# A Huber loss over 512 MB of inputs: eight added loads from GpSimd, and middle tiles computed in two pieces

## The chip, the cores and the metric

The kernel runs on one core of a Trainium2 chip. The metric is the device time of one execution in microseconds, as a median of several runs. TensorE does nothing here. The work is done by the DMA engines, which move data between HBM and the on-chip memory, by VectorE (DVE in the profile) and by ScalarE (ACT). SyncE (SP) issues the transfers; GpSimd (POOL) only sets four constants before the change.

## The reference

```python
def setup_inputs():
    return {"pred": np.random.randn(8192, 8192).astype(np.float32),
            "target": np.random.randn(8192, 8192).astype(np.float32)}

def reference(pred, target):
    delta = 1.0
    diff = pred - target
    abs_diff = np.abs(diff)
    return np.where(abs_diff <= delta, 0.5 * diff**2, delta * (abs_diff - 0.5 * delta))
```

Two inputs of 268 MB are read, one output of the same size is written, and each element needs a handful of operations.

## The kernel before

The arrays are taken as flat lists of 67 million numbers and cut into 40 tiles of 128 partitions. A tile has 13248 columns; the first and the last have 10432. One row of a full tile, 52992 bytes, lies contiguous in HBM. Two slots `a0`, `a1` hold `pred`, two slots `b0`, `b1` hold `target` and later the result; tile i uses slot i modulo 2.

For each piece of columns of a tile, VectorE subtracts (`a = a - b`, line 82) and clips (`b = clip(a, -1, 1)`, line 83), ScalarE then computes `b = Square(b * sqrt(0.5))` (line 86) and `a = |a|` (line 87), and VectorE ends with `b = max(a - 0.5, b)` (line 76). Since max(|d| - 0.5, clip(d)^2 / 2) is the Huber loss with delta 1, `b` then holds the result. The first halves of the pieces run ahead of the last step: `finish(2)` holds back the last step of two pieces. `PARTS` names the number of pieces of tiles 0 (two), 38 (four) and 39 (eight); all others, tiles 1 to 37, fall to the default in `shares(i, PARTS.get(i, 3))`, three pieces of 4416 columns.

All transfers are issued by SP in the order in which the program has them (`manual_schedule`): loads of tile 0, loads of tile 1, and then for each tile i its computation, `store(i)` (line 68) and the loads of tile i + 2 (line 49). A middle tile has one load of `a`, one of `b` and one store, 6624 KB each. Tiles 0 and 1 are loaded in halves of their columns (`HALVES`: a, b, a, b); the last two in smaller pieces. SP waits, in order, for what each transfer needs: the store of tile i for the last step of VectorE, the load of `a` for tile i + 2 until slot `a` is no longer read, the load of `b` for tile i + 2 until the store of tile i has left the slot. So while tile i is computed, the loads of tile i + 1 are under way.

Of the kernel before, what the change touches and what calls it, by code (L numbers as in the profile page):

```python
# [1 line left out]

# [4 lines left out]


@with_exitstack
def kernel(  # L10
    ctx: ExitStack,
    tc: tile.TileContext,
    pred: bass.AP,
    target: bass.AP,
    out: bass.AP,
):
    nc = tc.nc
    P = 128
    fp32 = mybir.dt.float32
    Alu = mybir.AluOpType  # L20
    Act = mybir.ActivationFunctionType
    SQRT_HALF = 0.70710678118654752

    total = pred.shape[0] * pred.shape[1] // P
    W = 13248

    ends = total % W + W
    widths = [ends - ends // 2] + [W] * (total // W - 1) + [ends // 2]
    n = len(widths)
    starts = [sum(widths[:i]) * P for i in range(n)]  # L30

    def block(x, i):
        flat = x.rearrange("r m -> (r m)")
        return flat[starts[i] : starts[i] + P * widths[i]].rearrange("(p m) -> p m", p=P)

    pool = ctx.enter_context(tc.tile_pool(name="slots", bufs=1))
    a_slots = [pool.tile([P, W], fp32, name=f"a{k}") for k in range(2)]
    b_slots = [pool.tile([P, W], fp32, name=f"b{k}") for k in range(2)]

    def shares(i, parts):  # L40
        w = widths[i] // parts
        edges = [k * w for k in range(parts)] + [widths[i]]
        return [slice(edges[k], edges[k + 1]) for k in range(parts)]

    def load(i, which, first, last):
        quarters = shares(i, 4)
        c = slice(quarters[first].start, quarters[last].stop)
        dst, src = (a_slots, pred) if which == "a" else (b_slots, target)
        nc.sync.dma_start(out=dst[i % 2][:, c], in_=block(src, i)[:, c])  # L49

    HALVES = (("a", 0, 1), ("b", 0, 1), ("a", 2, 3), ("b", 2, 3))
    LOADS = {
        0: HALVES,
        1: HALVES,
        n - 2: (("a", 0, 2), ("b", 0, 1), ("a", 3, 3), ("b", 2, 3)),
        n - 1: (("a", 0, 2), ("b", 0, 0), ("b", 1, 1), ("b", 2, 2), ("a", 3, 3), ("b", 3, 3)),
    }
    PARTS = {0: 2, n - 2: 4, n - 1: 8}

    def store(i):  # L60
        if i == n - 1:
            eighths = shares(i, 8)
            pieces = [slice(eighths[k].start, eighths[k + 1].stop) for k in (0, 2, 4)]
            pieces += eighths[6:]
        else:
            pieces = shares(i, 1)
        for c in pieces:
            nc.sync.dma_start(out=block(out, i)[:, c], in_=b_slots[i % 2][:, c])

    def compute(i):  # L70
        todo = []

        def finish(keep):
            while len(todo) > keep:
                a, b = todo.pop(0)
                nc.vector.scalar_tensor_tensor(  # L76
                    out=b, in0=a, scalar=-0.5, in1=b, op0=Alu.add, op1=Alu.max
                )

        for c in shares(i, PARTS.get(i, 3)):  # L80
            a, b = a_slots[i % 2][:, c], b_slots[i % 2][:, c]
            nc.vector.tensor_tensor(out=a, in0=a, in1=b, op=Alu.subtract)  # L82
            nc.vector.tensor_scalar(  # L83
                out=b, in0=a, scalar1=-1.0, scalar2=1.0, op0=Alu.max, op1=Alu.min
            )
            nc.scalar.activation(out=b, in_=b, func=Act.Square, scale=SQRT_HALF)  # L86
            nc.scalar.activation(out=a, in_=a, func=Act.Abs)  # L87
            todo.append((a, b))
            finish(2)
        finish(0)  # L90

    ctx.enter_context(tc.manual_schedule())

    def load_all(i):
        for piece in LOADS.get(i, (("a", 0, 3), ("b", 0, 3))):
            load(i, *piece)

    load_all(0)
    load_all(1)
    for i in range(n):  # L100
        compute(i)
        store(i)
        if i + 2 < n:
            load_all(i + 2)


# [1 line left out]
_INS = ['pred', 'target']  # L108
_OUTS = [((8192, 8192), 'float32')]


# [23 lines left out]
```

## Time and profile before

| | |
|---|---|
| time, median of 3 runs | 1868.83 us (1868.62 to 1869.63) |
| the profiled execution: its time, its span | 1869.48 us, 1867.7 us |
| VectorE busy | 1405.9 us, 75% |
| ScalarE busy | 903.7 us, 48% |
| SP's DMA queue, share of 16 engines' time | 99.8% |
| bytes read and written | 536.87 MB and 268.44 MB, 431 GB/s over the span |
| transfers | 134, all from SP |

In the profile a line is named by its number in the kernel, an engine and the tiles out<-in. `SPq` is SP's queue: a line with it is an issue of a transfer, not the transfer. "b<-in_target_dram" is a load of `target` into slot `b`, "out_dram<-b" a store. In the list of instructions in order of time, the columns are the start, the duration, the engine, the line and the operation, and in brackets the idle time before it and what ended it. In the chain of work that ended last the columns are start, duration and what stood on the chain, and the duration of a transfer runs from its issue to its landing, its time in the queue with it. A transfer is split by rows over the sixteen DMA engines, and each engine adds one to the transfer's semaphore when its share has landed: the trace has 16 such increments for each transfer, and their spread tells how far apart the engines are.

### The profile page before, as it was taken

Reading aid. Unit: us, or ns where it says so; the run is one execution under the profiler, and the core shown is the slowest. Engines: PE = TensorE matmul, PEld = TensorE weight load, DVE = VectorE, ACT = ScalarE, POOL = GpSimd, SP = SyncE. Lnnn points to the kernel's source line nnn. Section 1 sums busy time; section 2 is a strip of 40 time slices with the busy share of each in tenths; the row PEclk is TensorE's granted clock in tenths of the full one; section 3 lists DMA queues with packets and bytes.
Section 4 is the critical chain, followed back from the end, with each engine's and each line's share of the span. In section 5 each row is a group of like instructions: output and inputs, shape, how many; then the busy total and the mean of one; then the engine's idle time right before and its main releaser. Section 6 shows DMA issues by size and latency. Waiting matters only on the chain.

```text
span 1867.7 us, 983 instructions
## 1 busy us (share of the span) xinstructions
DVE 1405.9 (75%) x375; ACT 903.7 (48%) x251; POOL 0.2 (0%) x4
## 2 busy tenths in 40 slices
DVE  4877777777777777777777777777777777777796
ACT  4444444444444444444444444444444444444464
POOL 0000000000000000000000000000000000000000
DMA  9999999999999999999999999999999999999998
GB/s 410 432 429 434 432 436 433 435 433 431 431 436 431 436 434 436 435 431 431 434 434 435 435 435 436 435 429 434 434 431 436 434 435 436 435 429 435 430 428 377
DMA packets 19303, 805.37 MB, mean 431 GB/s; under 512 B 2144, under 2 KB 2144, under 8 KB 2400
## 3 DMA queue, kind: packets, MB, share of 16 engines
q1 hardware_dynamic: 19296, 805.31, 99.8%
q14 instruction: 7, 0.06, 0.0%
HBM read 536.87 MB, written 268.44 MB: 431 GB/s over the span
## 4 chain that ended last, share of the span: by engine, by line
DMA 60%; DVE 38%; issue 1%; ACT 0%; DVEq 0%; another core or an unknown queue 0%; SPq 0%
DMA b<-in_target_dram 32%; DMA out_dram<-b 28%; DVE a L82 15%; DVE b L76 15%; DVE b L83 8%; ACT b L86 0%; ACT a L87 0%; DVEq L130 0%; SPq L49 0%; DVEq L82 0%
## 5 line engine op out<-in xcount | busy, mean ns | idle before, releaser
L86 ACT ACTIVATE b<-b 128x4416 f32<-128x4416 f32 (+3 forms) x125 | 461.0, 3688 | 949.7 <-DVE b L83 949.7
L82 DVE TENSOR_TENSOR a<-a,b 128x4416 f32<-128x4416 f32 (+3 forms) x125 | 565.2, 4522 | 442.1 <-DMA b<-in_target_dram 442.1
L76 DVE SCALAR_TENSOR_TENSOR b<-a,b 128x4416 f32<-128x4416 f32 (+3 forms) x125 | 558.5, 4519 | 3.6 <-ACT a L87 3.6
L87 ACT ACTIVATE a<-a 128x4416 f32<-128x4416 f32 (+3 forms) x125 | 460.3, 3682 | 0.0
L83 DVE TENSOR_SCALAR b<-a 128x4416 f32<-128x4416 f32 (+3 forms) x125 | 293.0, 2344 | 4.3
L86 ACT ACT_TABLE_LOAD x1 | 1.3, 1283 | 0.7 <-PEq L119 0.7
L119 POOL MEMSET const-bfloat16-1.0<- 128x1 bf16 x1 | 0.1, 101 | 0.0
L119 POOL MEMSET const-uint8-127<- 128x1 uint8 x1 | 0.1, 101 | 0.0
L119 POOL MEMSET const-float32-0.0<- 128x1 f32 x1 | 0.1, 98 | 0.2 <-issue 0.2
L119 POOL MEMSET const-float32-1.0<- 128x1 f32 x1 | 0.1, 98 | 0.0
## 6 DMA issues: line engine op xcount, KB each, us to landing
out_dram<-b SPq DMA_DIRECT2D x38, 6624.0 KB, 26.9
a<-in_pred_dram SPq DMA_DIRECT2D x36, 6624.0 KB, 42.1
b<-in_target_dram SPq DMA_DIRECT2D x36, 6624.0 KB, 31.3
b<-in_target_dram SPq DMA_DIRECT2D x4, 3312.0 KB, 35.5
a<-in_pred_dram SPq DMA_DIRECT2D x2, 3312.0 KB, 40.5
a<-in_pred_dram SPq DMA_DIRECT2D x2, 2608.0 KB, 14.5
b<-in_target_dram SPq DMA_DIRECT2D x2, 2608.0 KB, 20.3
out_dram<-b SPq DMA_DIRECT2D x1, 5216.0 KB, 21.3
```

What stands on the lines that cost most here:

```text
L76: nc.vector.scalar_tensor_tensor(out=b, in0=a, scalar=-0.5, in1=b, op0=Alu.add, op1=Alu.max)
L82: nc.vector.tensor_tensor(out=a, in0=a, in1=b, op=Alu.subtract)
L83: nc.vector.tensor_scalar(out=b, in0=a, scalar1=-1.0, scalar2=1.0, op0=Alu.max, op1=Alu.min)
L86: nc.scalar.activation(out=b, in_=b, func=Act.Square, scale=SQRT_HALF)
L87: nc.scalar.activation(out=a, in_=a, func=Act.Abs)
L119: nc = _bacc.Bacc("TRN2", target_bir_lowering=False, num_devices=1)
```

## The change

GpSimd gets eight loads, issued by `ahead()` between the loads of tile 0 and those of tile 1. They come in four pairs. The first of a pair reads `low` rows of 16 columns (64 bytes a row), the second `16 - low` rows of 4096 columns (16384 bytes a row), with `low` 8, 10, 12 and 14. Their rows are four partitions apart, and no two of the eight touch the same bytes. They read `pred` for tile 1 into slot `a1`, the same data to the same place that the ordinary loads of tile 1 bring afterwards. Since those write the same bytes, SP now waits with its first load of `a` for tile 1 until the four loads of 4096 columns have landed, and with the second one for the four of 16 columns. The rest of SP's order is as it was.

Tiles 1 to 37 are computed in two pieces of 6624 columns in place of three of 4416, and `finish(1)` holds back the last step of one piece in place of two; tiles 38 and 39 keep their four and eight pieces, but there too a last step now comes one piece sooner in VectorE's order. Tile 0, with two pieces, keeps its order.

```diff
-        for c in shares(i, PARTS.get(i, 3)):
+        for c in shares(i, PARTS.get(i, 2)):
...
             todo.append((a, b))
-            finish(2)
+            finish(1)
         finish(0)
...
+    EXTRA = 4096
+
+    def ahead():
+        for low in (8, 10, 12, 14):
+            high = 16 - low
+            r = low // 2 - 4
+            for first, k, c in ((0, low, slice(W - 16, W)), (96 - 4 * high, high, slice(0, EXTRA))):
+                rows = slice(first + r, first + r + 4 * (k - 1) + 1, 4)
+                nc.gpsimd.dma_start(out=a_slots[1][rows, c], in_=block(pred, 1)[rows, c])
+
     load_all(0)
+    ahead()
     load_all(1)
```

## The prediction

> **What bounds the kernel now.** I read the page first. About 0.2% of 1868.83 us, 3.7 us, is what a measurement of this kernel can tell from no change.
>
> ```profile
> span 1867.7 us, 983 instructions
> DVE 1405.9 (75%) x375; ACT 903.7 (48%) x251; POOL 0.2 (0%) x4
> q1 hardware_dynamic: 19296, 805.31, 99.8%
> ```
>
> SP's queue fills the sixteen DMA engines for 99.8% of the span; VectorE is busy 75%. So the end is set by bytes and by how evenly the sixteen share them. Second, the chain, around one period of two tiles and around the slow early ones:
>
> ```profile
> 151.82 4.77 DVE a L82
> ...
> 246.99 4.77 DVE a L82
> ...
> 341.37 4.77 DVE a L82
> ...
> 435.52 4.77 DVE a L82
> ...
> 1222.72 26.86 DMA out_dram<-b
> 1249.59 31.27 DMA b<-in_target_dram
> 1280.95 4.77 DVE a L82
> ```
>
> One period is store 26.86, load of b 31.27, compute 35.6 (with issue gaps), together 93.85 us from 529 us on. That VectorE stands in this chain is no bound: a store takes 26.86 us only because its bytes wait behind a load; it is a third of a tile's 46.9 us of traffic, 15.6 us. The marks show something else: the first periods are 95.17, 94.38 and 94.15 us. Against 93.85 the slowest DMA engine loses 1.32 + 0.53 + 0.30 = 2.15 us there, then nothing. Two later stores take 27.66 and 27.67 us (from 846.52 and 1504.26) instead of 26.87: 0.8 us each.
>
> Third, the windows at the very end, busy time of all engines in each stretch (last columns: DMA share, GB/s):
>
> ```profile
> 1859.00:1861.00 2.00, 0.00 (x0) 0.00 (x0) 0.00 (x0) 1.00 0.99 404
> 1861.00:1861.50 0.50, 0.00 (x0) 0.00 (x0) 0.00 (x0) 1.00 0.60 240
> 1862.00:1862.50 0.50, 0.00 (x0) 0.00 (x0) 0.00 (x0) 1.00 0.31 125
> 1863.50:1864.00 0.50, 0.00 (x0) 0.00 (x0) 0.00 (x0) 1.00 0.23 94
> 1864.50:1865.00 0.50, 0.00 (x0) 0.00 (x0) 0.00 (x0) 1.00 0.05 21
> 1866.00:1866.50 0.50, 0.00 (x0) 0.00 (x0) 0.00 (x0) 1.00 0.03 10
> ```
>
> All sixteen work until 1861; from 1864.5 on a share of 0.05 is one engine in sixteen. The trace's semaphore increments, sixteen per transfer, say the same: their spread on the first input's loads is 0.65 us, 1.7 by 182 us, 3.0 by 307, 3.5 by 495, 4.5 after 870, 5.5 after 1495 and 5.5 on the last store. Ten engines end within 0.8 us of each other, six trail by 1.6, 2.9, 3.3, 3.5, 4.0 and 5.5. Following packets engine by engine, the trailers lost 0.1 to 0.7 us each time on the last row of a load of b while others turned to the store, until they stood some 2.8 us or more behind; then they lost almost nothing more. The last one also met three 8 KB instruction fetches (the second queue of the page), 0.7 to 0.8 us each, which explains the two long stores. If the work of 1861 to 1866.5 were levelled, it would end near 1862.3 (the shares sum to 1.3 us). So at most some 4 us can be won by levelling, and little beyond that: a row of 52992 bytes takes 1.956 us in nearly every record.
>
> **The change: GpSimd's loads.** The 44 rows of 64 bytes are nothing beside 52 KB rows: the nearest record, 5216 bytes, takes 0.20 us, so an engine with four of them pays between 0 and 0.8 us; by the order below the last pair of engines has none, so I take zero. The big ones are 8 + 6 + 4 + 2 = 20 rows of 16384 bytes, 0.33 MB. One row costs 16384 / 52992 x 1.956 = 0.61 us of one engine. The two transfers of each pair have 16 rows in all. If each row goes to another engine and the next transfer begins where the last ended, the small one takes engines 0 up to its count and the big one the rest: engines 8 and 9 get one big row, 10 and 11 two, 12 and 13 three, 14 and 15 four. That is a ramp of 0.61, 1.21, 1.82 and 2.42 us over eight engines, laid down before the first transition from load to store. The trace has no transfer on fewer than sixteen engines, so this is the assumption that counts; spread evenly the same bytes are 20 x 0.61 / 16 = 0.76 us on each. The Trainium skill ("DMA: Bandwidth & Descriptors", section "Why a DMA increments its semaphore by 16 and not by 1") says that GpSimd's transfers take a divisor of the row count as the number of engines, consecutive from a cursor that goes round, and knows an exception in which some copies use all sixteen; no transfer here can show which holds.
>
> Price of the ramp: the last pair carries 2.42 us of extra work to the end. What it buys: the slips of the trailing engines came while neighbours stood close, and engines far enough apart lost almost nothing for 1300 us. If the ramp does that from the start, the last engine trails by 2.42 plus what instruction fetches add. These become fewer: VectorE goes from 298 to 226 instructions and ScalarE from 253 to 179, SP stays at 131. I allow 0.4 us for one fetch half hidden (0 if it meets a leading engine, 0.8 if the last). So 5.5 us of trail becomes 2.42 + 0.4 = 2.8, a gain of 2.7. Bounds: at best the pack's own early losses go too (below); at worst the slips go on and the ramp adds to them, +2.4.
>
> Queues: the DMAs stand on GpSimd, which does only four memsets (0.2 us). SP's first load of a for tile 1 now waits for the four big ones, its third for the small ones, and SP is in order, so tile 1's b halves, store 0 and everything later are queued behind. The cover: tile 0's four loads keep the engines busy until about 27.7 us (their last increments), and an issue needs 1.2 us to its first packet (0.73 to 1.9 us at the start), so the wait is free if GpSimd's loads have landed by some 26.4 us; each us beyond costs one. SP's own issues take 0.34 to 0.70 us, eight make 2.8 to 5.6 us; 20 rows beside tile 0's rows add a few us at most. I take zero, with the upper end open until GpSimd's start is seen. By the Trainium skill's fit for GpSimd's transfers (same page, section "Anatomy of one DMA — SWDGE (gpsimd) path": 2.0 us each plus bytes), eight in a row would be an estimated 17 us, inside that cover too.
>
> **Two pieces instead of three.** Each of five groups loses 37 instructions, one for each of 37 tiles. From the rows of 4416 and 5216 columns (subtract 4.753 and 5.592, clip 2.459 and 2.876, Square 3.872 and 4.550, Abs 3.867 and 4.533, last step 4.750 and 5.589) a piece of 6624 costs 7.07, 3.61, 5.74, 5.71 and 7.07 us. One tile: subtract and clip to 10.7, ScalarE's first pair to 22.1, VectorE's second pair done at 21.4 (waits 0.8), last step to 29.2; ScalarE's second pair to 33.6, so VectorE waits 4.4; end at 40.7, against 35.6 now. This 5.1 us is on no path while the DMA queue has work:
>
> ```profile
> 1269.64 0.34 SPq L68 DMA_DIRECT2D out_dram<-b  x1
> 1280.95 4.76 DVE L82 TENSOR_TENSOR a<-a,b 128x4416 f32<-128x4416 f32 x1 [11.34 <-DMA b<-in_target_dram]
> ```
>
> The store is issued 11.3 us before the queue's last load lands; with two pieces 6.2 us, still above the 1.2 us of an issue. Gone, it would cost its lack 37 times; I take zero.
>
> The tail has less cover. There VectorE goes on from tile 37 to 38 without a wait (1786.51), and `finish(1)` adds waits for ScalarE: in tile 38 about 0.4 us at the first last step and 2.3 at the fourth (ScalarE's 5.9 us against one last step of 3.6), in tile 39 some 0.2 and 1.1. From the landing of tile 37's b to the last store's issue it is 104.9 us now (1751.01 to 1855.9), by such steps about 111.3 with the change, and 115.5 to the end of the DMA work (1866.5). So the last store, 0.65 MB, has 4.2 us left, and needs 1.2 us to its first packet and 1.6 for eight rows of 0.2: 1.4 us over. I take zero here too, but each us that I have missed beyond 1.4 is a us of time, up to perhaps 3.
>
> Sum: -5.5 + 2.4 + 0.4 = -2.7 us; I keep 0.2 of it back for the tail: -2.5. The profiled execution took 1869.48 us (span 1867.7, 1.8 around it), 0.65 above the median; there I expect a span near 1865.2. From the median: 1868.83 - 2.5 = 1866.3.
>
> **Rivals.** *The whole pack gains.* The leading engine also lost 0.6 us against its own best rows up to 490 us and 0.7 after. If the ramp removes the early slips for all and the last pair meets no fetch: -5.5 + 2.4 - 0.6 - 0.5 (part of the rest) = -4.2, 1864.6. For it: the losses fall on load-to-store turns that sixteen engines made together. Against: eight engines stay in step.
>
> *Tail bound by VectorE.* If the last issue comes 3 us later than worked out, the end moves by 1.6: 1867.9. The 15.6 us of loads that were still queued when tile 38's store was issued (1823.01) speak against a larger hole.
>
> *Bytes only.* GpSimd's rows spread over all engines, the slips stay: +0.76, 1869.6. By the Trainium skill ("DMA: Bandwidth & Descriptors", "Rules for kernel authors") issuing from another engine brings no bandwidth, and transfers under 64 KB are mostly overhead; the trace agrees that the queue is full, at 431 GB/s, but its last 5.5 us show that fullness is not level.
>
> *Ramp on top of slips.* The engines between 1 and 2.8 us behind were those hit; the ramp puts six there. Then 5.5 + 2.4, up to 1871.2.
>
> *GpSimd lands late.* Its first transfer has a start-up cost that no row shows. At 4.5 us for each of eight, they land at 37 us, 10.6 us past the cover: 1866.3 + 10.6 = 1876.9. It decides for slower from a landing at about 33 us (6.3 beyond cover). Against: 26 us are long beside SP's 0.7 us.
>
> **How the numbers follow.** Forecast 0.36; whole pack 0.32; tail 0.06; bytes only 0.03; ramp on top 0.03; late or another loss above 3.7 us 0.20. Faster by over 0.2% is the whole pack's case, 0.32; within it are forecast, tail, bytes and ramp on top, 0.48; slower 0.20. The range runs from 1863.6 (the pack's case with another us) to 1872.5, past the ramp on top; it leaves out most of the late case. The likeliest case's own range is 1865.1 to 1868.
>
> **What would show it.** Right: increments on tile 0's or 1's loads already 2 to 3 us apart and on the last store under 3.5; periods of 93.85 from the first; DMA share at 1.0 until some 2.5 us before the end; VectorE's wait for b near 6.3 us a tile; SP's first wait over before 26 us. Wrong: a spread at the end of 5 us or more, an idle DMA queue between 1855 and 1863, a gap in the DMA share near 28 us, or a wait for b near zero.

## The result and the profile after

The changed kernel takes 1880.87 us (median of 7 executions, 1870.47 to 1884.21) against 1868.83 us before (7 executions, 1868.26 to 1869.63): ratio 1.0058, 95% interval 1.0044 to 1.0071 (all ratios here come from all executions of a kernel, so they need not be the quotient of the two medians). It is slower, outside the forecast's range. Its executions differ by 14 us where those of before differ by 1.4, and the profiled one was the best of them, 1870.47 us. The same kernel run once more (`after_again` below) gave a profile of 1882.92 us, so both kinds can be read.

The page of the changed kernel, best execution:

```profile
span 1868.7 us, 818 instructions
DVE 1401.9 (75%) x264; ACT 896.9 (48%) x177; POOL 4.4 (0%) x12
q1 hardware_dynamic: 19296, 805.31, 99.8%
q0 software_dynamic: 256, 0.33, 0.1%
```

The queue is as full as before, 0.33 MB have come from GpSimd, and VectorE is no busier. Nothing on the page says what the other executions lose. The start, in order of time (start, duration, engine, line and operation), first VectorE's first line before, then the changed kernel:

```profile
15.86 5.59 DVE L82 TENSOR_TENSOR a<-a,b 128x5216 f32<-128x5216 f32 x1 [15.86 <-DMA b<-in_target_dram]
```

```profile
1.25 4.20 POOL L106 DMA_DIRECT2D a<-in_pred_dram  x8 [0.81 <-PEq L141]
...
19.81 5.59 DVE L82 TENSOR_TENSOR a<-a,b 128x5216 f32<-128x5216 f32 x1 [19.81 <-DMA b<-in_target_dram]
21.26 0.33 SPq L49 DMA_DIRECT2D a<-in_pred_dram  x1
```

GpSimd issues its eight loads in 4.2 us, and SP's wait for them is over at 21.26 us, ahead of the 26.4 us at which the queue would have run dry. But VectorE starts at 19.81 where it started at 15.86 before: the first two loads of tile 0 have landed 4 us later.

Now the place that the prediction had costed at nothing, store against next landing, around 1230 us of the best execution:

```profile
1228.66 0.34 SPq L68 DMA_DIRECT2D out_dram<-b  x1
1235.18 7.06 DVE L82 TENSOR_TENSOR a<-a,b 128x6624 f32<-128x6624 f32 x1 [6.55 <-DMA b<-in_target_dram]
```

The store is issued 6.5 us before the next load of b has landed, where it was 11.3; 6.2 had been worked out. Here it is enough. The chain of the long execution (`after_again`; start, duration, what) shows that it is not enough there:

```profile
289.27 22.05 DMA out_dram<-b
311.33 31.32 DMA b<-in_target_dram
...
950.50 22.20 DMA out_dram<-b
972.72 32.42 DMA b<-in_target_dram
...
1045.65 22.04 DMA out_dram<-b
1067.71 32.56 DMA b<-in_target_dram
...
1614.04 23.07 DMA out_dram<-b
1637.13 31.27 DMA b<-in_target_dram
```

A good period has a store of 22.05 and a load of 31.27 us. From 760 us on each period of two tiles is too long by 0.7 to 1.4 us, in the store or in the load; from 950.50 to 1045.65 it is 95.15 us, not 93.85. In the best execution all periods after 437 us take 93.84 to 94.41. The windows (length, busy time of the three engines, clock, DMA share, GB/s), first of the best execution, then of the long one, say the same:

```profile
673.00:860.00 187.00, 140.77 (x25) 90.25 (x16) 0.00 (x0) 1.00 1.00 434
1048.00:1235.00 187.00, 140.91 (x24) 90.25 (x16) 0.00 (x0) 1.00 1.00 433
1423.00:1611.00 188.00, 141.73 (x25) 90.25 (x16) 0.00 (x0) 1.00 1.00 434
```

```profile
110.00:485.00 375.00, 281.34 (x49) 180.50 (x32) 0.00 (x0) 1.00 1.00 434
673.00:860.00 187.00, 141.17 (x24) 90.25 (x16) 0.00 (x0) 1.00 1.00 430
1048.00:1235.00 187.00, 141.18 (x24) 90.25 (x16) 0.00 (x0) 1.00 1.00 429
1423.00:1611.00 188.00, 139.91 (x25) 90.25 (x16) 0.00 (x0) 1.00 1.00 428
```

The DMA share reads 1.00 in all of them: the engines count as busy, and yet move 1% less. So the share does not show the loss; the records of single rows do. The records carry no engine number: a row belongs to the engine whose row before it ended at that moment. The table has, for some tiles, the shortest time from the issue of a store to its first row on any engine, that is, how much queue the leading engine still had:

```
shortest time from a store's issue to its first row, us (profiled executions)
kernel            tile 10   tile 20   tile 30   tile 34   time of that execution
before              7.06      6.24      6.08      5.27    1869.48
after (best)        2.45      2.33      2.17      2.14    1870.47
after_again         2.39      1.59      0.90      0.93    1882.92
two_only            1.95      1.07      1.59      1.83    1881.71
```

About 0.85 us is the least that occurs in any run: then the engine had nothing left and waited for the store. One such place in the long execution, tile 16, whose store is issued at 808.39:

```profile
808.39 0.34 SPq L68 DMA_DIRECT2D out_dram<-b  x1
808.82 0.38 SPq L49 DMA_DIRECT2D a<-in_pred_dram  x1
815.16 7.06 DVE L82 TENSOR_TENSOR a<-a,b 128x6624 f32<-128x6624 f32 x1 [6.80 <-DMA b<-in_target_dram]
```

```profile
807.00:808.00 1.00, 1.00 (x1) 0.00 (x0) 0.00 (x0) 1.00 1.22 530
808.00:809.00 1.00, 0.36 (x1) 0.00 (x0) 0.00 (x0) 1.00 0.49 212
809.00:810.00 1.00, 0.00 (x0) 0.00 (x0) 0.00 (x0) 1.00 1.50 636
```

(A row counts in the slice in which it is recorded, so a share can pass 1.) By VectorE's line the store came 6.8 us ahead of the load's landing. But a landing is the sixteenth increment, that of the last engine. The leading engines were over 5 us ahead of it. The first of them was done with the load 0.54 us after the store's issue, and the first row of the store came 0.86 us after it; ten engines stood still, for 0.24 us on average. That is still the smaller part of the loss, as will be seen: most of it is in rows that take longer.

### The profile page after: what moved, and what is told of

It reads as the page before. It is cut to its first block, busy times and chain, and to the rows that moved or that the text cites. A ratio compares the mean times of both kernels' runs of the same rounds, so it can differ in the third digit from the quotient of the medians.

```text
span 1868.7 us, 818 instructions
## 1 busy us (share of the span) xinstructions
DVE 1401.9 (75%) x264; ACT 896.9 (48%) x177; POOL 4.4 (0%) x12
## 4 chain that ended last, share of the span: by engine, by line
DMA 53%; ACT 24%; DVE 21%; issue 2%; ACTq 0%; SPq 0%; DVEq 0%
DMA b<-in_target_dram 32%; DMA out_dram<-b 22%; ACT a L87 12%; ACT b L86 12%; DVE a L82 9%; DVE b L76 8%; DVE b L83 4%; SPq L49 0%; ACTq L141 0%; DVEq L82 0%; ACTq L87 0%; DVEq L83 0%
## 5 line engine op out<-in xcount | busy, mean ns | idle before, releaser
L86 ACT ACTIVATE b<-b 128x6624 f32<-128x6624 f32 (+3 forms) x88 | 454.2, 5161 | 963.3 <-DVE b L83 963.3
L82 DVE TENSOR_TENSOR a<-a,b 128x6624 f32<-128x6624 f32 (+3 forms) x88 | 559.7, 6360 | 266.3 <-DMA b<-in_target_dram 266.3
L76 DVE SCALAR_TENSOR_TENSOR b<-a,b 128x6624 f32<-128x6624 f32 (+3 forms) x88 | 560.0, 6363 | 191.2 <-ACT a L87 191.2
L87 ACT ACTIVATE a<-a 128x6624 f32<-128x6624 f32 (+3 forms) x88 | 453.4, 5152 | 0.0
L83 DVE TENSOR_SCALAR b<-a 128x6624 f32<-128x6624 f32 (+3 forms) x88 | 287.1, 3263 | 3.0
L106 POOL DMA_DIRECT2D a<-in_pred_dram x8 | 4.2, 533 | 0.8 <-PEq L141 0.8
```

The costliest lines, as they stand in the source:

```text
L76: nc.vector.scalar_tensor_tensor(out=b, in0=a, scalar=-0.5, in1=b, op0=Alu.add, op1=Alu.max)
L83: nc.vector.tensor_scalar(out=b, in0=a, scalar1=-1.0, scalar2=1.0, op0=Alu.max, op1=Alu.min)
L106: nc.gpsimd.dma_start(out=a_slots[1][rows, c], in_=block(pred, 1)[rows, c])
```

## The experiments

Each kernel was timed beside the kernel before on the same chip. "Cover" is the time by which a store is issued before the next load of b has landed.

**First: which half of the change.** `two_only` drops the call of `ahead()`; `ahead_only` keeps it and goes back to three pieces:

```diff
 # two_only                                # ahead_only
     load_all(0)                           -PARTS.get(i, 2) ... finish(1)
-    ahead()                               +PARTS.get(i, 3) ... finish(2)
```

> The two pieces alone, without GpSimd's loads. Theory L (in the timed runs GpSimd's loads land so late that SP's wait lets the DMA queue run dry before tile 1): 1867 to 1870, like before, since the wait is gone. Rival U (the added rows pile up on few DMA engines, which then trail by 10 us): the same, 1867 to 1870. Rival T (the two pieces cost it, in the steady cover or at the tail): 1878 to 1884.

> GpSimd's loads alone, three pieces as before. L and U: 1878 to 1884, all of the loss. T: 1866 to 1869.

`two_only`: 1881.71 us (1881.29 to 1882.94), ratio 1.0069 (1.0057 to 1.0081). `ahead_only`: 1870.70 us (1870.35 to 1871.02), ratio 1.0009 (1.0000 to 1.0018). The two pieces alone make the loss. GpSimd's loads alone cost 1.7 us, which puts `ahead_only` above the 1869 us at which T's range ended. Theory L, with which I had started from my rival of the late GpSimd, and U both fall here. Two more kernels agree. They vary GpSimd's loads and keep the two pieces:

```diff
 # second_half
-(96 - 4 * high, high, slice(0, EXTRA))
+(96 - 4 * high, high, slice(W - EXTRA, W))
 # tiny
-    EXTRA = 4096
+    EXTRA = 16
```

> The changed kernel, with the big rows put into the last 4096 columns of tile 1's slot, so that only the second load of a for tile 1 waits for GpSimd; two loads of 3312 KB (15.7 us of queue) go ahead of the wait. L: the queue no longer runs dry for 10 us, 1866 to 1871. U: the same rows on the same engines, 1878 to 1884. T: 1878 to 1884.

> The changed kernel with all eight GpSimd loads of 16 columns (64 bytes a row), so no ramp and no bytes, but the same eight transfers and the same two waits. L: the start-up and the eight transfers one after another stay, 1874 to 1884. U: nothing piles up, 1867 to 1870. T: 1878 to 1884.

`second_half`: 1879.97 us (1874.84 to 1885.14), ratio 1.0057 (1.0043 to 1.0072). `tiny`: 1882.01 us (1880.39 to 1882.76), ratio 1.0067 (1.0055 to 1.0079). Neither a later wait nor the absence of bytes helps, as T says and L (for the first) and U (for the second) do not.

The two costs do not add, though: 12.7 us and 1.7 us alone, but 12.0 us together (8.1 in `after_again`). And where the 16 KB rows are in, executions differ widely: of the 19 of the changed kernel and `second_half`, six took 1870 to 1876 us and thirteen 1879 to 1885. Without them, in `two_only` and `tiny`, all ten took 1880 to 1883. So the ramp seems to keep part of the loss away in some executions; none of them was below the median of the kernel before.

**Second: cover or width.** What the two pieces change is the cover (11.3 to 6.5 us in the shown places) and the width of the instructions. Four kernels part them; only `two_no_square` changes what is computed:

```diff
 # two_no_square (on two_only)
-            nc.scalar.activation(out=b, in_=b, func=Act.Square, scale=SQRT_HALF)
 # three_clip1, three_clip2 (on before; k < 1 and k < 2)
-        for c in shares(i, PARTS.get(i, 3)):
+        for k, c in enumerate(shares(i, PARTS.get(i, 3))):
...
+            if i not in PARTS and k < 2:
+                nc.vector.tensor_scalar(
+                    out=b, in0=a, scalar1=-1.0, scalar2=1.0, op0=Alu.max, op1=Alu.min
+                )
 # two_split (on two_only), in store
-            pieces = shares(i, 1)
+            pieces = shares(i, 1 if i == 0 or i == n - 2 else 2)
```

> The two pieces alone, without the square of line 86 (left out, so ScalarE does only the absolute value). VectorE's instructions keep their 6624 columns, but the computation of a tile takes 35.5 us instead of 40.7, so the store is issued 11.4 us before the next load of b has landed, as in the kernel before. Theory C (the store and the next load are issued too late for the leading DMA engines, which run some 5 us ahead of the last one): the loss goes, 1867 to 1871. Rival W (the wider instructions of VectorE disturb the transfers): 1878 to 1884.

> The kernel before with three pieces, and the clip of line 83 done twice on the first piece of each middle tile (the same result): 2.5 us more for VectorE, the cover falls from 11.3 to 8.9 us. C: still above the 5.5 us of spread and the 1.2 us of an issue, 1868 to 1870. W: 1868 to 1870.

> As the one before, with the clip done twice on the first two pieces: 4.9 us more, the cover falls from 11.3 to 6.4 us, as in the changed kernel, but with the narrow instructions of three pieces and no GpSimd. C: all of the loss, 1877 to 1884. W: 1868 to 1870.

> The two pieces alone, with the store of tiles 1 to 37 in two halves, each issued when its piece is done; the first half then stands in the queue some 17 us before the last load lands. Rows of half the size cost about 8 ns more for two, and one more increment: 2 to 3 us in all. C: 1869 to 1873. W: 1878 to 1886.

| kernel | cover, us | us | ratio (95%) |
|---|---|---|---|
| two_no_square | 11.6 | 1868.76 (1868.05 to 1869.38) | 0.9999 (0.9990 to 1.0009) |
| three_clip1 | 8.8 | 1870.10 (1869.30 to 1870.68) | 1.0006 (0.9996 to 1.0015) |
| three_clip2 | 6.3 to 7.9 | 1882.32 (1879.18 to 1884.10) | 1.0070 (1.0055 to 1.0085) |
| two_split | first half of a store much earlier | 1871.61 (1871.28 to 1872.72) | 1.0016 (1.0007 to 1.0025) |

Three of the four lie in the range of theory C, and `three_clip1` 0.1 us above it; its 1.4 us over the kernel before are not clear of no change (interval 0.9996 to 1.0015), and where they arise stays open. W falls: wide instructions with the old cover lose nothing, narrow ones with the new cover lose everything. `two_split` is the changed computation in full, and gets nearly all back by splitting the store, at the 2 to 3 us of the smaller rows. Two lines of order of time from `two_no_square`, then two of the chain of `three_clip2`:

```profile
1221.84 0.34 SPq L68 DMA_DIRECT2D out_dram<-b  x1
1233.47 7.06 DVE L82 TENSOR_TENSOR a<-a,b 128x6624 f32<-128x6624 f32 x1 [11.67 <-DMA b<-in_target_dram]
```

```profile
1046.90 21.88 DMA out_dram<-b
1068.80 32.48 DMA b<-in_target_dram
```

The first has its 11.6 us between issue and landing with instructions of 6624 columns; the second has the stretched load, 32.48 in place of 31.27, without any of them. In the rows, the shortest time from issue to first row stays at 6.9 us or more in `two_no_square` and at 3.48 or more in `three_clip1`, and is 0.84 to 1.85 in `three_clip2` from tile 7 on.

**Third: the threshold, and the spread of executions.** `after_again` is the changed kernel. `three_clip15` repeats the clip on one piece and a half:

```diff
 # three_clip15 (on three_clip2)
+                h = slice(0, 4416 if k == 0 else 2208)
-                    out=b, in0=a, scalar1=-1.0, ...
+                    out=b[:, h], in0=a[:, h], scalar1=-1.0, ...
```

> The changed kernel once more, to get a profile of it that has the loss, if it comes. Theory C in its sharper form: rows are stretched, and time is lost, from the tile on in which the first DMA engines reach the end of a load less than some 2 us after the store was issued; the first profile stayed above that (2.1 us at the least) and took 1870.47. C: 1878 to 1884 in most executions; where the profile is slow, the time from a store's issue to its first packet goes to 0.8 to 2 us, and where it is not, it stays above 2. Rival V (the GpSimd loads' landing differs from run to run): the loss lies before 60 us.

> Three pieces, the clip done twice on the first piece and on half of the second (the same result): 3.8 us more for VectorE, cover 7.6 us, between the 8.9 us that cost 1.4 us and the 6.4 us that cost 13.6. C: with a spread of up to 5.5 the shortest time from issue to first packet ends near 2.3 us, so most executions are still whole, 1869 to 1873; one that meets one more instruction fetch tips over late. A loss in proportion to the cover taken away would give 1875 to 1877.

`after_again`: 1876.96 us (1869.96 to 1882.92 in 6 executions), ratio 1.0043 (1.0021 to 1.0064). The wait for GpSimd ends at 20.88 us in the long profile, so the loss does not lie there (rival V falls). Three of the six executions are in the 1878 to 1884 us that were expected of most. The shortest time in the long profile is 2.4 us at tile 10, 1.8 at tile 12 and 1.4 at tile 14, and it is from tile 14 on that rows are stretched (by over 0.1 us) in every tile, on nine or more of the sixteen engines. `three_clip15`: 1870.15 us (1869.23 to 1878.17 in 10 executions), ratio 1.0016 (1.0005 to 1.0027). Five executions are within 1869.2 to 1869.7, two lie at 1877 and 1878. The profile is one of the late ones: above 2.8 us until tile 14, below 2.0 from tile 16 on, stretched rows on nine engines or more from tile 20 on. In the best profile of the changed kernel the number never falls below 2.1. So the loss is not in proportion to the cover. It comes on at some 2 us of queue left on the leading engine, and once on it stays.

**Fourth: GpSimd's 1.7 us.** Three pieces, and `EXTRA = 16` (`three_tiny`) or 2048 (`three_ramp_half`):

> Three pieces and GpSimd's eight loads, all of 64-byte rows. If the 16 KB rows make the 1.7 us that GpSimd's loads cost by themselves: 1868.4 to 1869.2, and a spread of the first loads as before (0.65 us). If the eight transfers and the two waits make it: 1870 to 1871.

> Three pieces and GpSimd's loads with 8 KB rows in place of 16 KB, so a ramp of 1.2 us in place of 2.4 and half the bytes. If the bytes stretch the ordinary rows of all engines meanwhile (2.1 us on each in the run with 16 KB rows) and the slips go on as before: half the cost, 1869.2 to 1870.2. If a ramp of this size keeps the slips away at half the price: 1867 to 1868.5.

`three_tiny`: 1868.75 us (1867.66 to 1869.41), ratio 0.9998 (0.9989 to 1.0008). `three_ramp_half`: 1868.92 us (1868.35 to 1870.70), ratio 1.0000 (0.9991 to 1.0010). The eight transfers and the two waits cost nothing that can be seen; the 16 KB rows make the 1.7 us. Half the ramp costs less than half of that, between its two expectations; it brings nothing either.

No run points to a version that beats the kernel before.

## Why the prediction was wrong

**The step that failed is the cover of the two pieces.** It read: "The store is issued 11.3 us before the queue's last load lands; with two pieces 6.2 us, still above the 1.2 us of an issue. [...] I take zero." The piece times were right (7.06, 3.61, 5.72, 5.71, 7.06 us against 7.07, 3.61, 5.74, 5.71, 7.07), and so was the cover (6.5). The comparison was wrong: 6.2 us is the reserve of the engine that lands last. The prediction had itself measured that ten engines end 4.7 to 5.5 us ahead of that one. Their reserve is 6.2 less the spread, 1 to 3 us, and the runs show that rows stretch from about 2 us downwards. The two facts stood some paragraphs apart and were not subtracted from each other.

**The price was wrong as well.** "Gone, it would cost its lack 37 times" allows a loss only once the cover is gone, and then only as an idle queue. Measured is about 1 us per period of two tiles once the reserve of the leading engines is small, about 13 us over the whole kernel (`two_only`), and hardly any of it is idle time: the rows of SP's queue took 1876.2 us per engine in the profiled execution of `two_only`, against 1864.1 before, 12.1 more, while the span grew by 11.9. The records say which rows: the ten or eleven leading engines lose up to 1.1 us each on the last row of a store and on the first of the next load, the trailing ones up to 1.3 on one of the last two rows of a load of b. The spread does not pass some 5.8 us there. That the loss of the leading engines lets the others catch up, and that engines in step are those that slip, as in the first periods of before, is my reading; what stretches a row on a busy engine is not seen in the trace, and stays open.

**Why executions differ.** Whether the spread stays under about 4 us hangs on a few slips, as I read the two profiles of the changed kernel. In the best one it did not pass 3.8 us until 1700 us; in the long one it grew to 5.7 by 768. The instruction fetches do not tell the two apart by number or time: both have them at 347, 536 and 623 us. But the one at 536 met the last engine in the long profile (spread from 3.63 to 4.14 us) and the last but one in the best (3.51 to 3.68), and from 640 us on rows without a fetch slipped in the long one.

**The ramp had the size that was worked out, by another path, and bought little.** Increments of tile 0's fourth load are 2.58 us apart, 2.42 were forecast. But the order assumed for it, the 64-byte rows of a pair on some engines and its 16 KB rows on the others, did not happen. Starts of the first pair's rows in `ahead_only`:

```
rows of 64 bytes   5.434 5.475 5.547 5.600 5.633 5.736 5.759 5.880
rows of 16 KB      6.990 7.032 7.103 7.156 7.189 7.293 7.315 7.436
```

Each of the 16 KB rows starts 1.556 or 1.557 us after one of the 64-byte rows, which is two ordinary rows of 0.775 us and the small records between them: it is on the same engine. So the two transfers of this pair start at the same engine; if the later pairs start there too, those of 8, 6, 4 and 2 rows lie on top of each other and make the same ramp. That its size came out all the same is luck.

The Trainium skill ("DMA: Bandwidth & Descriptors", section "Why a DMA increments its semaphore by 16 and not by 1") states an exception in which some of GpSimd's copies are spread over all sixteen engines, with a sixteenth of the rows, rounded up, on each. With one row to an engine, this pair fits that exception, and not the cursor as the prediction applied it.

Two things were missed about the price. While the 16 KB rows ran, every engine's ordinary rows were longer: tile 0's loads took 27.7 us per engine in `ahead_only` against 25.6 before, 2.1 us that no engine gets back (0.8 with the 8 KB rows of `three_ramp_half`). And the slips went on: the spread in `ahead_only` rose from 2.5 to 3.8 by 570 us and to 4.8 at the end. So 5.5 us of trail became 4.8, not 2.8, and 2.1 came on top: +1.4 by this sum, +1.7 measured. That lies between the rivals "bytes only" (1869.6) and "ramp on top of slips" (1871.2).

**Readings that were off without changing the sum.** The pages have VectorE at 375 instructions before and 264 after, and ScalarE at 251 and 177, not 298 and 226, 253 and 179; they have 7 records of instruction fetches before and 6 after. The first row of the run starts 1.0 us after the first issue, not 1.2, and 0.84 is the least in any run.

**The rivals.** The result is inside "late or another loss above 3.7 us", but not by its mechanism. GpSimd's loads landed at 21 us, five before the limit worked out, and tile 0's loads kept every engine busy until 30 us, so the wait left no gap. The Trainium skill's fit ("DMA: Bandwidth & Descriptors", "Anatomy of one DMA — SWDGE (gpsimd) path") gave an estimated 17 us for eight; the trace has the last landing at about 21.2 us, 19.9 after the first issue.

**The tail** was right: in the best profile the leading engines wait some 2 us in all for the last stores, the trailing ones never, and the last issue still stands before the end of the trailing engines' work.

## What to carry to other kernels

A semaphore that waits for all sixteen increments tells of the last DMA engine; a full queue is needed on the first. Before a cover is spent, subtract the spread of the increments from it, and leave some 2 us over that; where the rest is of the size of one slip, time several executions, because one profile can show the lucky case. A DMA share of 1.00 does not show that the stores come too late: look at GB/s over equal periods, or at the time from an issue to its first row.

## What was not expected of the hardware

- Rows on busy engines become longer when a store comes late: 52992 bytes take 1.956 us as a rule, and up to 3.3 us in `two_only`.
- The effect has a threshold, at some 2 us on the leading engine, and stays on: in ten executions of one kernel (`three_clip15`) eight are at 1869 to 1873 us and two at 1877 to 1878, and in the profile of one of these two rows are stretched in every tile from 20 on.
- GpSimd's transfers of 20 rows of 16 KB made the ordinary rows longer, by 2.1 us per engine on average, where their bytes are 0.76 us per engine; with rows of 64 bytes (`three_tiny`) no such cost is seen.
